# Hybrid state space and sparse attention block: the gated projection in another order, all state space products ahead of the attention products

## The chip, the cores and the metric

The kernel runs on one core of a Trainium2 chip. The metric is the device time of one execution in microseconds (us). A profile of one execution shows, for every engine, when its instructions ran and what they waited for: TensorE (PE), VectorE (DVE), ScalarE (ACT), GpSimd (POOL), and SyncE (SP), which here issues all DMA transfers in one queue.

## The reference

One decoder block over 2048 tokens of width 1024. A state space branch (S5) and a sparse attention branch (an indexer picks 256 keys per query) start from the same normalised input. Their outputs, 512 wide each, are projected to 1024, gated, added and projected again; a SwiGLU feed-forward part follows.

```python
y_ssm = _s5_branch(u, ...)                       # 2048 x 512
y_att = _dsa_branch(q, k, v, qi, ki, wi)         # 2048 x 512
g_ssm, g_att = jnp.split(gates, N_BRANCH, axis=-1)
merged = (jax.nn.sigmoid(g_ssm) * (y_ssm @ w_proj_ssm[l])
          + jax.nn.sigmoid(g_att) * (y_att @ w_proj_attn[l]))
x = x + merged @ w_out[l]
h2 = _rms(x, norm2_g[l])
x = x + (jax.nn.silu(h2 @ w_ffn_gate[l]) * (h2 @ w_ffn_up[l])) @ w_ffn_down[l]
```

## The kernel before

**Who sets the order.** Three Python generators write the program: `state` (the state space branch), `attention` (16 query tiles of 128, with the top-k search ahead of them) and `dense` (everything behind the branches). `Pace.run` asks whichever can go on first by its own model of the engines, so the three are woven into one order for each engine. That order is fixed when the program is built; at run time each engine takes its rows in that order and waits where a row needs another engine. All instructions are recorded by one helper, so the profile gives each of them line 206: they are told apart by the names of their tiles.

**Dense blocks.** `dense` handles four blocks (`tb` 0 to 3) of 512 tokens, each in `block`. Its stages are: the projection, 16 products of 12 matmuls (fp32 as a high and a low half, three matmuls for each of four depth slices), called P1 to P16 here; the output stage, `f<-ww,mg`, 192 matmuls; the normalisation and its turning (transposes `f<-ident,ha` and so on); then up, gate and down, `f<-h,ww` and `f<-wd,at`, 1664 matmuls. A product of the projection takes the ssm branch's tile `act0` or the attention branch's `act1` (four pieces of 512 KB each, stored to DRAM by the branches, loaded by `load_branch`) and a weight item `ww`. Before, a weight item holds the columns of one output tile for both branches. The products come in the order ssm, ssm, attention, attention for tiles 0 and 1, and then ssm and attention by turns.

**Merging.** For each product DVE multiplies the PSUM result with its gate (`scalar_tensor_tensor`, in the profile `g<-g,f`; called a scaling here). Gates `g0` and `g1` are loaded from DRAM (`g<-gate`, 256 KB), two buffers of each kind. Behind the second scaling of a tile, POOL or DVE adds the two (`g<-g,g`), ACT casts the high half (`mg<-g`) and DVE or POOL makes the low half (`mg<-g,mg`). The output stage reads `mg`: its k-th pair of tiles is first needed 12 k matmuls after its start.

**Weights.** Block 0 loads raw weights (`raw`, two buffers), ACT casts the high half, POOL or DVE makes the low half (`ww<-raw,ww`), and the pair is stored as `wc`. Blocks 1 to 3 load `wc` items (1 MB, `ww<-wc`) into four buffers; a load waits until TensorE has finished with the item that had the buffer.

**Attention and the blocks.** `self.attended` counts finished query tiles. Block `tb` waits, before it is written, until 4 (tb + 1) of them are finished. At the end of a block the next block's `act0` is loaded, and `act1` too if its attention is already finished; that is so for blocks 1 and 2, not for block 3.

**PSUM.** A block has a pool `psp` of 3 banks, and borrows 4 that attention leaves free at times (`spare_banks`, `bank`); the last block, when attention is over, has 8 of its own.

**DMA.** SP issues every transfer in program order and cycles through eight completion counters, so a transfer also waits for the one issued eight before it.

## Time and profile before

| | |
|---|---|
| median of three runs | 3360.59 us (3353.09 to 3363.12) |
| the profiled execution | 3357.88 us |
| its span, first to last instruction | 3355.8 us |
| TensorE busy in the span | 3171.5 us, 95% |
| DVE, ACT, POOL busy | 2106.4, 1275.1, 638.1 us (63%, 38%, 19%) |
| DMA, mean over the span | 180 GB/s |

The profiled execution is one run, so a sum of its parts is compared with its own 3357.88 us; the last 2 us are outside the span. A busy TensorE is not one at its peak: its instructions take longer when the clock granted to it is lower. In the rows below, a row of the timeline gives the start in us, the duration in us, the engine, the operation, the tiles written and read, how many such instructions stand together (xN), and in brackets how long the engine idled before it and on what it waited.

### The profile page before, as it was taken

The page shows a single profiled execution, that of the slowest core. Times are in us where ns is not written, and L with a number is a line of the kernel's source. Part 1 is how long each engine was busy: PE and PEld are TensorE (multiplying, and loading weights), DVE is VectorE, ACT ScalarE, POOL GpSimd, SP SyncE. Part 2 cuts the span into 40 slices and gives each one's busy share as a digit, 9 for nine tenths or more (in the row PEclk, how much of TensorE's full clock was granted, in tenths as well). Part 3 has the DMA queues.
Part 4 walks back from the last instruction along what each step waited for, and adds up shares of the span by engine and source line. Part 5 has one row for each costly group of instructions (what it writes and reads, how often), then busy time and mean ns, then how long its engine had stood idle before and what let it go on. Part 6 is the DMA issues. An engine that isn't in the chain of part 4 may idle for free. (4 is left out here: it accounts for less than half of the span.)

```text
span 3355.8 us, 42712 instructions
## 1 busy us (share of the span) xinstructions
PE 3171.5 (95%) x15528; PEld 2651.1 (79%) x15528; DVE 2106.4 (63%) x4532; ACT 1275.1 (38%) x2211; POOL 638.1 (19%) x628
## 2 busy tenths in 40 slices
PE   7999989899977999989999999999999999999999
PEld 6988767678755788877778888877888888788887
DVE  6555685555587766688687775876886666422223
ACT  3231544445552444346322443665314444210000
POOL 4323676522223311234100000001000000000000
PEclk9999999999988999999999999999999999999999
DMA  5743333534447775656847324366555332755543
GB/s 184 227 122 109 121 89 108 164 120 142 129 166 268 283 257 196 237 182 225 332 187 262 109 93 166 140 236 242 197 213 182 119 108 88 268 195 219 207 177 149
DMA packets 312961, 605.56 MB, mean 180 GB/s; under 512 B 46352, under 2 KB 194608, under 8 KB 282032
## 3 DMA queue, kind: packets, MB, share of 16 engines
q1 hardware_dynamic: 312752, 602.85, 51.7%
q8 instruction: 122, 2.00, 0.2%
q14 instruction: 87, 0.71, 0.1%
HBM read 434.70 MB, written 166.89 MB: 179 GB/s over the span
## 5 line engine op out<-in xcount | busy, mean ns | idle before, releaser
L206 PE MATMUL f<-h,ww 128*128 128x512 f32 (+1 forms) x4416 | 1013.1, 384 | 1.3 <-DVE h L206 0.8
L206 PEld LDWEIGHTS f<-h,ww 128*128 128x128 f32 x4416 | 803.4, 191 | 156.5 <-DVE h L206 1.8
L206 PE MATMUL f<-wd,at 128*128 128x512 f32 x2112 | 518.2, 397 | 28.7 <-DVE t L206 6.5
L206 PEld LDWEIGHTS f<-wd,at 128*128 128x128 f32 x2112 | 396.3, 191 | 116.5 <-DVE t L206 8.1
L206 PE MATMUL gps<-hT,gw 128*128 128x512 f32 x1536 | 387.5, 403 | 4.6 <-ACT gsg L206 3.2
L206 ACT ACTIVATE jka<-S,tr 128x1920 bf16<-128x1920 f32 (+6 forms) x217 | 305.6, 1408 | 180.5 <-DVE tr L206 128.7
L206 PEld LDWEIGHTS gps<-hT,gw 128*128 128x128 f32 x1536 | 288.3, 193 | 68.5 <-ACT gsg L206 5.2
L206 PE MATMUL mm<-w,hT 128*128 128x512 f32 (+1 forms) x1152 | 282.8, 403 | 10.3 <-DVE hT L206 7.2
L206 DVE TENSOR_TENSOR x<-f,x 128x512 f32<-128x512 f32 x352 | 235.1, 686 | 77.0 <-PE f L206 76.4
L206 PEld LDWEIGHTS mm<-w,hT 128*128 128x128 f32 x1152 | 241.5, 239 | 36.7 <-DVE hT L206 8.6
L206 DVE TENSOR_TENSOR tl<-pt,th 128x512 fp32r<-128x512 f32 (+1 forms) x288 | 183.8, 658 | 120.9 <-ACT th L206 119.8
L206 DVE SCALAR_TENSOR_TENSOR t<-t,f 128x512 f32<-128x512 f32 (+1 forms) x123 | 82.1, 668 | 271.8 <-PE f L206 223.6
L206 ACT CAST th<-pt 128x512 fp32r<-128x512 f32 (+1 forms) x288 | 155.5, 563 | 223.8 <-PE pt L206 220.2
L206 PE MATMUL f<-act,ww 128*128 128x512 f32 x768 | 191.8, 411 | 29.5 <-POOL ww L206 20.4
L206 PEld LDWEIGHTS f<-act,ww 128*128 128x128 f32 x768 | 151.2, 199 | 69.5 <-POOL ww L206 24.2
L206 POOL TENSOR_TENSOR g<-g,g 128x512 f32<-128x512 f32 x31 | 39.8, 1285 | 793.9 <-DVE g L206 793.9
L206 PE MATMUL f<-ww,mg 128*128 128x512 f32 x768 | 180.3, 397 | 10.6 <-ACT ww L206 7.0
L206 ACT ACTIVATE P<-P,m 128x1024 f32<-128x1024 f32 (+7 forms) x192 | 172.3, 900 | 46.9 <-DVE m L206 46.8
L206 PE MATMUL lg<-kk,q 128*128 128x512 f32 (+1 forms) x640 | 183.3, 388 | 3.5 <-DMA kk<-kk 3.5
L206 ACT ACTIVATE t<-f 128x512 f32<-128x512 f32 (+1 forms) x92 | 52.9, 575 | 343.8 <-PE f L206 343.7
L206 PEld LDWEIGHTS f<-ww,mg 128*128 128x128 f32 x768 | 147.2, 192 | 43.2 <-ACT ww L206 7.9
L206 ACT CAST at<-t 128x512 fp32r<-128x512 f32 (+1 forms) x92 | 55.2, 600 | 325.4 <-DVE t L206 325.3
(361 smaller groups left out, 4497.9 us busy)
## 6 DMA issues: line engine op xcount, KB each, us to landing
ww<-wc SPq DMA_DIRECT2D x180, 1024.0 KB, 4.9
wd<-wc SPq DMA_DIRECT2D x66, 1024.0 KB, 7.2
wc<-ww SPq DMA_DIRECT2D x60, 1024.0 KB, 7.5
raw<-in_w_in_dram SPq DMA_DIRECT2D x104, 256.0 KB, 3.4
wc<-wd SPq DMA_DIRECT2D x22, 1024.0 KB, 6.3
x<-in_x_dram SPq DMA_DIRECT2D x32, 512.0 KB, 5.3
gate<-gsg SPq DMA_DIRECT2D x64, 256.0 KB, 2.2
g<-gate SPq DMA_DIRECT2D x64, 256.0 KB, 5.7
```

Source lines behind the costliest of these rows:

```text
L206: return f(*args, **kw)
```

## The change

The weight items of the projection are regrouped: an item now holds two output tiles' columns of one branch, four items for the ssm branch and then four for the attention branch. The 16 products follow in that order: q = 0 to 7 are the ssm products, whose scalings write into `x1` (as `kept`), a tile that is free until the residual input is loaded into it; q = 8 to 15 are the attention products, each followed by its scaling, the addition of `kept`, and the split into `mg`. The wait for this block's attention moves from the block's start to q = 8; at its start a block only waits for the attention of the blocks before it. `act1`, where it has not been loaded before, is loaded at q = 6 if attention is finished when that place is written, else at q = 8. The loads of the residual `x1` move to q = 9, 11, 13 and 15. Every block has 3 own banks; once attention is over, the last block borrows 5 more, which `bank` gives out for short uses only. The depth of the ring of down weights, `nd`, is computed where the ring is made, with the same values.

```diff
--- before.py
+++ after.py
@@ -1663,11 +1663,12 @@
 
         a = self.a
         items = []
-        for ct in range(KD):
-            items.append(("w", lambda raw, ct=ct: [
-                (raw[:, i * 512:(i + 1) * 512].rearrange("p (k c) -> p k c", k=4),
-                 a[w][0, :, ct * 128:(ct + 1) * 128].rearrange("(k p) c -> p k c", p=128))
-                for i, w in enumerate(("w_proj_ssm", "w_proj_attn"))]))
+        for w in ("w_proj_ssm", "w_proj_attn"):
+            for c0 in range(0, KD, 2):
+                items.append(("w", lambda raw, w=w, c0=c0: [
+                    (raw[:, i * 512:(i + 1) * 512].rearrange("p (k c) -> p k c", k=4),
+                     a[w][0, :, (c0 + i) * 128:(c0 + i + 1) * 128].rearrange("(k p) c -> p k c", p=128))
+                    for i in range(2)]))
         for half in range(2):
             for q in range(4):
                 items.append(("w", lambda raw, half=half, q=q: [
@@ -1692,7 +1693,7 @@
             self.nc.sync.dma_start(z[:, :, k].bitcast(F32), (self.act_d, self.att_d)[br][tb][:, :, k])
         return z
 
-    def block(self, tb, bigp, ld, nps, nd):
+    def block(self, tb, bigp, ld):
 
         nc, a, at = self.nc, self.a, self.pace.at
         n = TB
@@ -1701,7 +1702,7 @@
         hf, h0 = t0 // HALF, t0 % HALF
         spare = self.pace.spare
         with ExitStack() as st:
-            psp = self.pool(st, "fps", nps, PSUM)
+            psp = self.pool(st, "fps", 3, PSUM)
             x1 = self.pool(st, "x1", 1).tile([128, nt, D], F32, name="x1")
 
             more, extra = ExitStack(), []
@@ -1744,34 +1745,49 @@
                     self.pace.tight = tb == 0
                     load_gate(0, 0)
                     act = self.act
-                    act += [self.load_branch(bigp, br, tb) for br in range(len(act), 2)]
+                    if not act:
+                        act.append(self.load_branch(bigp, 0, tb))
                     self.act = []
                     load_gate(1, 0)
-                    load_gate(0, 1)
-                    load_gate(1, 1)
-                    for q, (ct, br) in enumerate([(0, 0), (1, 0), (0, 1), (1, 1)] +
-                                                 [(ct, br) for ct in range(2, KD) for br in range(2)]):
-                        w = ld.get("w", 1 if q == 1 else 0)
-                        w = w.rearrange("p z a (b k c) -> p (z a) b k c", b=2, k=4)[:, :, br]
+
+                    kept = x1.rearrange("p t (a c) -> p (t a) c", a=2)
+                    for q in range(2 * KD):
+                        br, ct = q // KD, q % KD
+                        if q == KD:
+                            if self.attended < 4 * (tb + 1):
+                                yield lambda: at("PE") if self.attended >= 4 * (tb + 1) else ("PE", 1e9, None)
+                            if self.attended == NT:
+                                self.pace.BIAS = 0.0
+                                self.spare_banks = 5
+                        if q == KD - 2 or q == KD:
+
+                            if len(act) == 1 and self.attended >= 4 * (tb + 1):
+                                act.append(self.load_branch(bigp, 1, tb))
+                            if q < KD:
+                                load_gate(0, 1)
+                                load_gate(1, 1)
+                        w = ld.get("w")
+                        w = w.rearrange("p z a (b k c) -> p (z a) b k c", b=2, k=4)[:, :, ct % 2]
                         yield ready(w, act[br])
                         ps = bank()
                         for k in range(4):
                             self.mm3(ps, w[:, 0, k], w[:, 1, k], act[br][:, 0, k], act[br][:, 1, k], k == 0, k == 3)
                             ld.tick()
-                        x = gates[ct, br]
-                        nc.vector.scalar_tensor_tensor(x, x, 1.0, ps, op0=ALU.add, op1=ALU.mult)
-                        if br == 1:
+                        x = gates.pop((ct, br))
+                        if br == 0:
+                            nc.vector.scalar_tensor_tensor(kept[:, ct], x, 1.0, ps, op0=ALU.add, op1=ALU.mult)
+                        else:
+                            nc.vector.scalar_tensor_tensor(x, x, 1.0, ps, op0=ALU.add, op1=ALU.mult)
+                            spare(x).tensor_tensor(x, x, kept[:, ct], op=ALU.add)
+                            self.split(x, mg[:, 0, ct], mg[:, 1, ct], nc.scalar, spare(x))
+                        load_gate(ct + 2, br)
+                        if ct % 2 == 1:
                             ld.drop("w")
-                            x0, x = gates.pop((ct, 0)), gates.pop((ct, 1))
-                            spare(x0).tensor_tensor(x0, x0, x, op=ALU.add)
-                            self.split(x0, mg[:, 0, ct], mg[:, 1, ct], nc.scalar, spare(x0))
-                            load_gate(ct + 2, 0)
-                            load_gate(ct + 2, 1)
+                            if br == 1:
+                                t = ct // 2
+                                nc.sync.dma_start(x1[:, t], a["x"][0, t0 + t * 128:t0 + (t + 1) * 128])
                         if q == 3:
                             self.pace.tight = False
-                        if q in (4, 6, 8, 10):
-                            t = q // 2 - 2
-                            nc.sync.dma_start(x1[:, t], a["x"][0, t0 + t * 128:t0 + (t + 1) * 128])
                 fn = self.pool(sm, "fn", 1)
                 gB = fn.tile([128, D], F32, name="gB")
                 self.bcast_row(gB, a["norm2_g"], D)
@@ -1860,6 +1876,7 @@
                 self.pace.tight = False
             ap = self.pool(st, "fa", 5)
             tp = self.pool(st, "ft", 2)
+            nd = 2 if self.attended == NT else 1
             ld.ring("d", self.pool(st, "fd", nd), nd, 2)
 
             def gate(p):
@@ -1986,11 +2003,9 @@
                 for tb in range(NB):
                     if tb == 1:
                         first.close()
-                    yield lambda: self.pace.at("PE") if self.attended >= 4 * (tb + 1) else ("PE", 1e9, None)
-                    alone = self.attended == NT
-                    if alone:
-                        self.pace.BIAS = 0.0
-                    yield from self.block(tb, bigp, ld, *((8, 2) if alone else (3, 1)))
+                    if self.attended < 4 * tb:
+                        yield lambda: self.pace.at("PE") if self.attended >= 4 * tb else ("PE", 1e9, None)
+                    yield from self.block(tb, bigp, ld)
 
         st = ExitStack()
         pr = self.pool(st, "spr", 1)
```

TensorE has as many instructions as before; DVE has 9 more, ACT 4 more and POOL 13 fewer.

**Block 3 on SP.** Before, the last stores of attention (`att3`), a first gate, and the four loads of `act1` stand together, ahead of the block's fifth weight item `ww_25522<-wc4`:

```order
L206 DMA att3_189<-yh_25440 128x4x128 [waits DMAHW2_49,Activation_49]
L206 DMA att3_189<-ya_24339 128x4x128 [waits DMAHW3_49,DVE_49]
L206 DMA g0_25467<-gate0_1_135 128x512 [waits DMAHW4_49,PE_49]
L206 DMA act1_25469<-att3_189 128x2x512 [waits DMAHW5_49,DMAHW3_49,DMAHW2_49]
L206 DMA act1_25469<-att3_189 128x2x512 [waits DMAHW6_49]
L206 DMA act1_25469<-att3_189 128x2x512 [waits DMAHW7_49]
L206 DMA act1_25469<-att3_189 128x2x512 [waits DMAHW0_49]
L206 DMA g0_25474<-gate1_1_137 128x512 [waits DMAHW1_49]
L206 DMA g1_25476<-gate8_1_151 128x512
L206 DMA g1_25478<-gate9_1_153 128x512
L206 DMA ww_25522<-wc4_9257 128x2048 [waits DMAHW4_49,PE_49]
```

In the changed program the block has begun when attention ends. Around the same stores and loads SP's rows are these (gates of tiles 6 to 9, and the items `wc6` and `wc7`):

```order
L206 DMA g0_25540<-gate6_1_147 128x512 [waits DMAHW7_49,DVE_49]
L206 DMA g0_25559<-gate7_1_149 128x512 [waits DMAHW0_49,DVE_49]
L206 DMA ww_25561<-wc6_9259 128x2048 [waits PE_49]
L206 DMA g1_25563<-gate8_1_151 128x512
L206 DMA g1_25565<-gate9_1_153 128x512 [waits DMAHW6_49]
L206 DMA att3_189<-yh_25542 128x4x128 [waits Activation_49]
L206 DMA att3_189<-ya_24339 128x4x128
L206 DMA ww_25605<-wc7_9260 128x2048 [waits DMAHW1_49,PE_49]
L206 DMA act1_25607<-att3_189 128x2x512 [waits DMAHW7_49,DMAHW2_49,DMAHW0_49]
L206 DMA act1_25607<-att3_189 128x2x512 [waits DMAHW3_49]
L206 DMA act1_25607<-att3_189 128x2x512 [waits DMAHW4_49]
L206 DMA act1_25607<-att3_189 128x2x512 [waits DMAHW5_49]
```

The stores have moved behind the load of g0_25559, which waits for DVE (the scaling of P6 frees its buffer), and the `act1` loads behind ww_25605, which waits for TensorE to finish P8.

**Block 1 on DVE.** Before, two scalings stand ahead of each low half `mg`, here for two of the middle tiles of the block:

```order
L206 TENSOR_TENSOR mg_14512<-g0_14574,mg_14512 128x512
L206 SCALAR_TENSOR_TENSOR g0_14597<-g0_14597,f_14639 128x512
L206 SCALAR_TENSOR_TENSOR g1_14599<-g1_14599,f_14654 128x512
L206 TENSOR_TENSOR mg_14512<-g0_14597,mg_14512 128x512
L206 SCALAR_TENSOR_TENSOR g0_14635<-g0_14635,f_14677 128x512
L206 SCALAR_TENSOR_TENSOR g1_14637<-g1_14637,f_14692 128x512
```

In the changed program's second half, with attention products only, these are the first four tiles:

```order
L206 SCALAR_TENSOR_TENSOR g1_14619<-g1_14619,f_14659 128x512
L206 TENSOR_TENSOR mg_14506<-g1_14619,mg_14506 128x512
L206 SCALAR_TENSOR_TENSOR g1_14621<-g1_14621,f_14678 128x512
L206 TENSOR_TENSOR mg_14506<-g1_14621,mg_14506 128x512
L206 SCALAR_TENSOR_TENSOR g1_14676<-g1_14676,f_14700 128x512
L206 TENSOR_TENSOR mg_14506<-g1_14676,mg_14506 128x512
L206 SCALAR_TENSOR_TENSOR g1_14695<-g1_14695,f_14719 128x512
L206 TENSOR_TENSOR mg_14506<-g1_14695,mg_14506 128x512
```

Each low half has moved between two scalings: a scaling now stands behind the low half of the tile before it.

**Block 0 on DVE, the top-k search.** Rows on `jkd`, `uf` and `tf` are the search of later query tiles, six rows an iteration. Before, in the middle of the projection, they lie between the scalings singly and in part iterations:

```order
L206 SCALAR_TENSOR_TENSOR g0_9500<-g0_9500,f_9598 128x512
L206 TENSOR_SCALAR jkd_7800<-H4_8577,tf2_7816 128x320
L206 SCALAR_TENSOR_TENSOR jkd_7800,cnt2_7815<-H4_8577,tf2_7816,jkd_7800 128x320
L206 SCALAR_TENSOR_TENSOR g1_9502<-g1_9502,f_9615 128x512
L206 TENSOR_TENSOR mg_9369<-g0_9500,mg_9369 128x512
L206 SCALAR_TENSOR_TENSOR g0_9588<-g0_9588,f_9643 128x512
L206 TENSOR_SCALAR jkd_7800<-H5_8579,tf2_7816 128x384
L206 SCALAR_TENSOR_TENSOR jkd_7800,cnt2_7815<-H5_8579,tf2_7816,jkd_7800 128x384
L206 TENSOR_SCALAR uf2_7817<-cnt2_7815 128x2
L206 SCALAR_TENSOR_TENSOR tf2_7816<-uf2_7817,tf2_7816 128x2
L206 SCALAR_TENSOR_TENSOR g1_9590<-g1_9590,f_9662 128x512
L206 TENSOR_TENSOR g0_9588<-g0_9588,g1_9590 128x512
```

In the changed program five iterations stand together between the last ssm scaling (`x1_9352<-g0_9530,f_9564`, 31 rows above these) and the first attention scaling. This is the fifth, and what follows it:

```order
L206 TENSOR_SCALAR jkd_7800<-H4_8577,tf2_7816 128x320
L206 SCALAR_TENSOR_TENSOR jkd_7800,cnt2_7815<-H4_8577,tf2_7816,jkd_7800 128x320
L206 TENSOR_SCALAR jkd_7800<-H5_8579,tf2_7816 128x384
L206 SCALAR_TENSOR_TENSOR jkd_7800,cnt2_7815<-H5_8579,tf2_7816,jkd_7800 128x384
L206 TENSOR_SCALAR uf2_7817<-cnt2_7815 128x2
L206 SCALAR_TENSOR_TENSOR tf2_7816<-uf2_7817,tf2_7816 128x2
L206 SCALAR_TENSOR_TENSOR g1_9537<-g1_9537,f_9623 128x512
L206 TENSOR_TENSOR mg_9356<-g1_9537,mg_9356 128x512
L206 SCALAR_TENSOR_TENSOR g1_9539<-g1_9539,f_9648 128x512
L206 TENSOR_TENSOR g1_9539<-g1_9539,x1_9352 128x512
```

The search rows have moved out from between the scalings and stand in one stretch ahead of the attention half.

## Rows read from the trace of the kernel before

**Rows 1.** Waits of TensorE over the whole span by what it waited for: us in total, times, longest us.

```profile
PE f L206 <- POOL ww L206: 23.9, 11, 9.5
PE f L206 <- ACT ww L206: 11.8, 5, 4.6
PE f L206 <- DMA act<-att: 4.4, 4, 2.1
```

**Rows 2.** Busy time by stretch, for the projection of blocks 0, 1, 2 and 3. Columns: stretch, its length, busy us (and instructions) of PE, PEld, DVE, ACT and POOL, granted clock as a share of full speed, DMA share, GB/s.

```profile
980.80:1051.70 70.90, 55.35 (x192) 40.43 (x192) 51.46 (x111) 16.21 (x24) 29.23 (x16) 0.87 0.86 292
1621.90:1665.60 43.70, 43.70 (x194) 36.18 (x193) 15.94 (x25) 5.64 (x9) 9.02 (x7) 1.00 0.94 361
2247.30:2291.00 43.70, 43.70 (x194) 36.18 (x193) 15.68 (x23) 4.35 (x7) 9.01 (x7) 1.00 0.91 342
2884.90:2942.20 57.30, 51.08 (x203) 40.62 (x202) 18.14 (x28) 4.97 (x8) 8.98 (x7) 0.91 0.82 296
```

**Rows 3.** Timeline of PE from the end of block 2 to the output stage of block 3.

```profile
2879.31 5.62 PE L206 MATMUL f<-wd,at 128*128 128x512 f32 x24
...
2886.81 1.97 PE L206 MATMUL lg<-r,hsel 8*128 8x128 f32 x8 [1.78 <-DVE r L206]
2888.71 8.25 PE L206 MATMUL f<-act,ww 128*128 128x512 f32 x24
2898.07 0.96 PE L206 MATMUL f<-act,ww 128*128 128x512 f32 x3 [1.12 <-DMA act<-att]
...
2904.28 37.94 PE L206 MATMUL f<-act,ww 128*128 128x512 f32 x159 [0.36 <-DMA act<-att]
2942.06 3.11 PE L206 MATMUL f<-ww,mg 128*128 128x512 f32 x13
```

**Rows 4.** Timeline of SP, which issues the transfers, at the start of block 3.

```profile
2890.19 0.38 SPq L206 DMA_DIRECT2D att<-yh  x1
...
2893.90 2.50 SPq L206 DMA_DIRECT2D act<-att  x4
```

**Rows 5.** Timeline of PE in block 0's projection and output stage.

```profile
980.81 5.53 PE L206 MATMUL f<-act,ww 128*128 128x512 f32 x12 [9.54 <-POOL ww L206]
...
1020.57 5.30 PE L206 MATMUL f<-act,ww 128*128 128x512 f32 x22 [0.58 <-POOL ww L206]
...
1056.29 0.79 PE L206 MATMUL f<-ww,mg 128*128 128x512 f32 x1 [4.57 <-ACT ww L206]
...
1074.57 37.03 PE L206 MATMUL f<-ww,mg 128*128 128x512 f32 x155 [1.93 <-POOL ww L206]
```

**Rows 6.** Busy time of the first part of block 0's projection, columns as in rows 2.

```profile
980.80:1020.00 39.20, 31.23 (x98) 22.20 (x98) 26.81 (x60) 10.89 (x17) 16.17 (x9) 0.80 0.90 312
```

**Rows 7.** Timeline of DVE in block 3's projection: a scaling, the low half behind the second scaling of a tile, the next scaling.

```profile
2909.62 0.69 DVE L206 SCALAR_TENSOR_TENSOR g<-g,f 128x512 f32<-128x512 f32 x1 [0.19 <-PE f L206]
2912.42 0.69 DVE L206 TENSOR_TENSOR mg<-g,mg 128x512 fp32r<-128x512 f32 x1 [2.12 <-ACT mg L206]
2913.03 0.68 DVE L206 SCALAR_TENSOR_TENSOR g<-g,f 128x512 f32<-128x512 f32 x1
```

**Rows 8.** The gate tiles of block 1 (projection and output stage): time of their transfers from issue to landing.

```profile
DMA to landing us min/median/max: 2.8/6.2/7.5
```

**Rows 9.** Timeline of DVE in block 1's projection.

```profile
1659.89 1.31 DVE L206 SCALAR_TENSOR_TENSOR g<-g,f 128x512 f32<-128x512 f32 x2 [0.97 <-DMA g<-gate]
1663.32 0.69 DVE L206 TENSOR_TENSOR mg<-g,mg 128x512 fp32r<-128x512 f32 x1 [2.12 <-ACT mg L206]
1665.00 1.34 DVE L206 SCALAR_TENSOR_TENSOR g<-g,f 128x512 f32<-128x512 f32 x2 [0.99 <-DMA g<-gate]
```

**Rows 10.** Timeline of PE in the turning of the normalised rows and the first up product, of block 1 (the first two rows) and of block 3 (the last two): where the turning starts, and the first matmuls after it.

```profile
1709.88 1.09 PE L206 MATMUL f<-ident,ha 128*128 128x128 f32 x8 [0.75 <-DVE ss L206]
...
1723.12 12.21 PE L206 MATMUL f<-h,ww 128*128 128x256 f32 x80
...
2985.58 1.03 PE L206 MATMUL f<-ident,ha 128*128 128x128 f32 x8
...
2994.50 15.71 PE L206 MATMUL f<-h,ww 128*128 128x256 f32 x102
```

**Rows 11.** Timeline of SP at the start of block 0.

```profile
979.66 4.94 SPq L206 DMA_DIRECT2D act<-att  x4
984.83 2.06 SPq L206 DMA_DIRECT2D g<-gate  x3
987.29 0.38 SPq L206 DMA_DIRECT2D raw<-in_w_proj_ssm_dram  x1
```

**Rows 12.** Timeline of POOL in block 0's projection: a low half of weights and an addition of two scaled products.

```profile
1002.34 2.35 POOL L206 TENSOR_TENSOR ww<-raw,ww 128x1024 fp32r<-128x1024 f32 x1
1004.64 1.29 POOL L206 TENSOR_TENSOR g<-g,g 128x512 f32<-128x512 f32 x1
```

**Rows 13.** Timeline of DVE in the search: the same operation in two iterations that follow on each other, and in one beside POOL's row of 1002.34 us.

```profile
969.69 0.30 DVE L206 TENSOR_SCALAR jkd<-H,tf 128x320 bf16<-128x320 uint16 x1
...
972.17 0.30 DVE L206 TENSOR_SCALAR jkd<-H,tf 128x320 bf16<-128x320 uint16 x1
...
1002.33 2.47 DVE L206 TENSOR_SCALAR jkd<-H,tf 128x320 bf16<-128x320 uint16 x1
```

## The prediction, made before the changed kernel was timed

> **What bounds the kernel now.** I read four views, in this order. First the page: TensorE is busy 95% of the span, so only what makes TensorE wait can pay. Second, TensorE's waits by cause: of the waits that this change could touch, 23.9 us are for weights that POOL splits, 11.8 us for weights that ACT casts, and only 4.4 us for the attention branch's tiles [rows 1]. Third, the projection stage of each of the four blocks [rows 2]. Blocks 1 and 2 take 43.70 us with TensorE busy for 43.70 of them: nothing is waited for, and 43.70 / 192 = 0.2276 us is one matmul at full rate. Block 0 takes 70.9 us and block 3 57.3 us. Fourth, the timeline of those two.
>
> In block 3 attention ends just as block 2 does: its last rows stand at 2886.81 us, the first 24 matmuls of the projection take 8.25 us, the four pieces of the attention tile then let three matmuls through at a time, and from 2904.28 us all runs through [rows 3]. From 2884.9 us (2879.31 + 5.62) to 2942.06 us that is 57.2 us for 192 x 0.2276 = 43.7 us of products and some 1.5 us of attention: **about 12 us are lost there**, the largest loss that the change addresses. The tile's loads are issued at 2893.90 us, after attention's stores at 2890.19 us [rows 4], and the first products that need it start at 2898.07 us, the last piece is there at 2904.28 us [rows 3]: 4.2 us from first issue to first use, and 6.2 us from the first piece to the last.
>
> In block 0 the projection starts at 980.81 us, behind a wait of 9.54 us, is half done (98 matmuls) at 1020.0 us [rows 5, 6], and the stage that follows is free of weight waits from 1074.57 us on [rows 5].
>
> **Block 3: the wait moves.** The new order puts P1 to P8 (the ssm products) ahead of the attention tile. They start at 2884.9 us, take 96 x 0.2276 = 21.9 us and let attention's last eight matmuls in (1.97 us in [rows 3], about 1 us at full rate): P8 ends near 2907.9 us. What the order of SP shows decides the rest. Attention's stores now stand behind the gate load g0_25559, which waits for a result of P6, and the tile's loads behind ww_25605, which waits for P8 to release its weights. So they can't be issued before 2907.9 us, 14 us later than now. The first piece is usable 4.2 us later, or 2.9 us more when the 1 MB of ww_25605 goes ahead (1.05 MB at the 361 GB/s of [rows 2]): 2912.1 to 2915.0 us. The last piece comes 6.2 us behind, P9 ends 0.9 us after that, at 2919.2 to 2922.1 us, and seven products of 2.73 us end P16 at 2938.3 to 2941.2 us, against 2942.06 us [rows 3]: -0.9 to -3.8, and I take **-2**. The idle time ahead of P9 becomes one wait of 4 to 7 us in place of several short ones. The first 12 matmuls of block 0 took 5.53 us behind their 9.54 us wait [rows 5], 0.461 us each, the lower of the two clock levels (1.2 and 2.4 GHz); against 0.2276 that is 2.8 us more. P9 is paced by the pieces anyway, so I charge none of it; if P10 pays it, the term is +0.8.
>
> The Trainium skill speaks against the change here: "TensorE: Matmul & The Clock Gate", section "HAM oscillation — how this bites in real kernels", says that matmuls that come in bursts with a transfer waited for between them fall back to the slow clock and pay at each burst. By that rule block 3's term is the +0.8; the trace agrees in kind, by the 5.53 us of [rows 5].
>
> **Attention half, blocks 1 to 3: a chain in place of cover.** Now DVE scales two products per output tile, and POOL's addition, ACT's cast and DVE's low half follow once per 24 matmuls (5.46 us). In the new order that chain follows each of P9 to P16, every 2.73 us, and DVE's next scaling stands behind the low half of the one before. From one scaling to the next that order takes 3.41 us (2909.62 to 2913.03 us) [rows 7]. The gate tiles add to it: two buffers serve the attention half, and a tile is free only after the low half, so two products take max(6.82, 3.41 + L), where L is a gate load: 2.8, 6.2 and 7.5 us (least, median, most) in block 1 [rows 8], where scalings already wait for gates [rows 9]. The eighth merged tile is then ready 3 x max(6.82, 3.41 + L) + 6.9 us after P9. TensorE hides it until P16's end (7 x 2.73 = 19.1) and 39 matmuls of the output stage (8.9): 28.0 us. With L = 2.8 that is 27.4 us, no loss; with 6.2 it is 35.7 us, a loss of 7.7. L was measured while DMA moved 361 GB/s [rows 2]; the new chain spreads the same 2 MB over 7.9 us in place of 5.46, so I take L = 4.5: 30.6 us, a loss of 2.6, with a slower clock behind it **+3 in each of the three blocks**. Blocks 1 and 2 have no wait to set against it. The scalings of the ssm half write elsewhere and free their gate at once, so their two buffers take 0.7 + L per two products: with L = 6.2 that is 1.4 us behind per pair, 4.3 us by the last, less than the two products (5.46 us) by which three banks let TensorE run ahead.
>
> **Last block's banks.** Own banks go from 8 to 3, and the five borrowed ones serve neither the turning of the normalised rows nor the first up product. That passage takes 8.9 us in block 3 now (2985.58 to 2994.50) and 13.2 us in block 1 (1709.88 to 1723.12), which has 3 own banks and the search beside it [rows 10]. So 0 to +4.3; I take **+2**, as half of block 1's difference looks like the search.
>
> **Block 0.** The ssm half no longer stands behind the attention tile's loads, which now hold SP from 979.66 us for 4.94 us and put the next raw weights at 987.29 us [rows 11]. It is also rid of POOL's share in the merging, one addition of 1.29 us per output tile and at times a low half; the weights' own low halves, 2.35 us twice per item, fit into 5.46 us of products [rows 12]. P1 to P8 could then end at 980.81 + 5.53 + 84 x 0.2276 + some 6 us of remaining weight waits (an estimate) = 1011.5 us instead of 1020.0, and P9 starts at about 1016, when its tile has come behind the last ssm gates. But the order of DVE puts five iterations of the top-k search between the last ssm scaling and the first attention scaling: 2.48 us each when alone (969.69 to 972.17), 2.2 us more for each POOL split that meets one (2.47 against 0.30 us) [rows 13], so 12.4 to 16.8 us. The first attention scaling so falls at 1026 to 1030 us, and eight tiles of 3.4 us or more end at 1054 to 1058 us. The weights, all of which must still be split, hold the output stage as now. At best its last item starts at 1058, 16 us before 1074.57 us [rows 5], and the search that was left behind takes 2 back: -14. At worst the late merging costs more than the front gave, +3. I take **-5**, nearer to the worse end since [rows 1] names the weights.
>
> The added instructions themselves cost nothing on TensorE (as many as before); DVE has 9 more, ACT 4 more, POOL 13 fewer.
>
> **Sum.** -5 + 3 + 3 + (3 - 2 + 2) = +4 on the profiled 3357.9 us: 3361.9 us. That execution lies 2.7 us under the median of 3360.59 us, by less than the sum is good for; the forecast is **3362 us, no measurable change**. A measurement here tells 0.3% from nothing, 10 us to each side: 3350.5 to 3370.7.
>
> **Rivals.**
> 1. *Faster: block 0 keeps its front.* If the weight split follows the faster start, block 0 gives -14, and with L below 3.4 us the chain costs nothing: 3357.9 - 14 - 2 + 2 = 3344 us. For it: POOL was busy for only 29 of block 0's 71 us [rows 2]. Against it: the search on DVE. Chance 0.24, with block 3's tile coming early as a lesser way.
> 2. *Slower: the gate loads set the pace.* With L at 6.2 us or more the attention half loses 7.7 us in each of three blocks: 3357.9 - 5 + 3 x 7.7 - 2 + 2 = 3376 us. It decides from L = 5.5 us, where the three losses come to 17 us. For it: the median of [rows 8] lies above that. Against it: a stalled TensorE asks for less. Chance 0.28.
> 3. *Nothing but the place of the wait.* Block 3 loses before P9 what it lost before P1, blocks 0 to 2 break even: 3358 us. Within the forecast's bounds, 0.12 of its 0.46.
> 4. *The clock falls in block 3's long wait*: +2.8, 3365 us, 0.1 of the 0.46. With late banks as well it goes over 3371, 0.02, counted as slower.
>
> **How the numbers follow.** Forecast and its variants 0.46; faster 0.24; slower 0.28 + 0.02 = 0.30. The outermost tenth on each side is left out: 3344 to 3378 us, from the first rival to a little past the second. The forecast's own range is 3352 to 3370.
>
> **What would show it.** Block 3: loads of the attention tile issued after 2907 us and a wait of 4 to 7 us ahead of P9; wrong if they are issued before P8's end. Blocks 1 and 2: the output stage waits for the merged tiles on DVE or ACT, 1 to 5 us, and scalings 3.4 us or more apart; wrong if the output stage waits for nothing. Block 0: P8's end near 1012 and the last weight wait of the output stage near 1067 instead of 1074.57 us. The prediction fails if the search after block 0, once shifted, holds attention 4 to 7 back, or if waits appear in the feed-forward products, of which I assumed no change.

## The result, and the profile after

The changed kernel takes 3384.84 us (median of 4 runs, 3383.59 to 3389.05) beside 3357.55 us for the kernel before: ratio 1.0083, 95% interval 1.0063 to 1.0102. It is slower by 27 us; the forecast was 3362 us, 3344 to 3378, so the measured time lies above the whole range. The profiled execution took 3384.3 us, 26.4 us above that of before. TensorE's work is the same (15528 matmuls, 3171.0 us busy against 3171.5), so all of it is waiting.

Where it went, read from the starts of TensorE's rows in both timelines (a stage ends where the next one's first matmul starts):

| us, changed less before | forecast | measured |
|---|---|---|
| start of block 0 | 0 | +1.1 |
| block 0: projection | | -11.6 |
| its output stage | | +10.9 |
| its turning, up to the first uninterrupted up products | | +7.5 |
| the rest of block 0 | | +1.2 |
| block 0 in all | -5 | +7.9 |
| block 1 | +3 | +5.7 |
| block 2 | +3 | +5.3 |
| block 3: projection, from the end of block 2's down products | -2 | +0.6 |
| block 3: output stage | +3 | +4.2 |
| block 3: turning, with fewer own banks | +2 | +1.4 |
| sum | +4 | +26.3 |

The projection of the four blocks in the windows view (stretch, its length, busy us of PE, PEld, DVE, ACT and POOL, granted clock, DMA share, GB/s), to be set beside [rows 2]:

```profile
981.90:1042.80 60.90, 49.34 (x192) 37.70 (x192) 31.46 (x88) 12.98 (x19) 22.90 (x11) 0.87 0.89 306
1631.00:1674.70 43.70, 43.70 (x193) 36.20 (x194) 13.70 (x25) 7.28 (x11) 6.42 (x5) 1.00 0.74 270
2262.10:2305.80 43.70, 43.70 (x194) 36.19 (x193) 13.07 (x24) 7.19 (x9) 6.42 (x5) 1.00 0.75 268
2904.90:2962.90 58.00, 48.40 (x203) 38.16 (x202) 15.89 (x25) 3.73 (x6) 6.49 (x6) 0.91 0.71 247
```

In this stage blocks 1 and 2 are as before and block 0 is 10 us shorter: only in block 3 does the stage whose order was changed lose anything itself. TensorE's timeline in block 3 (start, duration, xN, and in brackets the wait ahead):

```profile
2904.86 8.45 PE L206 MATMUL f<-act,ww 128*128 128x512 f32 x36
2913.24 1.11 PE L206 MATMUL lg<-r,hsel 8*128 8x128 f32 x8
2914.27 13.87 PE L206 MATMUL f<-act,ww 128*128 128x512 f32 x60
2937.24 3.15 PE L206 MATMUL f<-act,ww 128*128 128x512 f32 x6 [9.10 <-issue]
2940.56 21.88 PE L206 MATMUL f<-act,ww 128*128 128x512 f32 x90 [0.17 <-DMA act<-att]
...
2970.99 39.71 PE L206 MATMUL f<-ww,mg 128*128 128x512 f32 x168 [2.53 <-DMA ww<-wc]
```

P1 to P8 now run with one row of attention among them, as forecast; then TensorE stands for 9.10 us, where 4 to 7 were forecast. SP at that place:

```profile
2925.25 0.55 SPq L206 DMA_DIRECT2D att<-yh  x1
2925.84 0.58 SPq L206 DMA_DIRECT2D att<-ya  x1
2928.17 0.33 SPq L206 DMA_DIRECT2D ww<-wc  x1
2932.80 2.49 SPq L206 DMA_DIRECT2D act<-att  x4
```

The loads (`act<-att`) are not issued when P8 releases its weights (`ww<-wc`, 2928.17 us) but 4.6 us later: they wait for attention's stores (`att<-yh`, `att<-ya`), issued at 2925.25 and 2925.84 us and landed at 2932.0 and 2932.8 us, 6.8 to 6.9 us after issue. TensorE's row names no releaser (`issue`); the first piece of the tile landed at 2937.16 us, and the matmuls start at 2937.24 us. Before, the same stores were issued at 2890.19 and the loads that wait for them at 2893.90 us [rows 4].

The clock falls behind the wait. Stretches ahead of it and behind it, columns as above:

```profile
2914.30:2928.10 13.80, 13.80 (x61) 11.15 (x60) 4.65 (x7) 0.62 (x1) 0.00 (x0) 1.00 0.83 298
2937.20:2940.50 3.30, 3.15 (x6) 1.67 (x6) 0.00 (x0) 0.00 (x0) 0.00 (x0) 0.50 0.99 342
2940.50:2946.00 5.50, 5.44 (x19) 4.28 (x20) 0.69 (x1) 0.42 (x1) 1.28 (x1) 0.76 0.07 25
2946.00:2962.50 16.50, 16.44 (x73) 13.29 (x71) 6.38 (x10) 2.69 (x5) 5.12 (x4) 1.00 0.65 234
```

From full clock ahead of the wait TensorE falls to 0.50 (1.2 GHz), and in the last stretch it is back at 1.00. P9 to P16 take 25.5 us in place of 21.85, but most of that is not the clock's price. P9's matmuls start in threes as the four pieces of the tile land, at 2937.16, 2938.70, 2940.52 and 2941.80 us (the row of 2940.56 us waits for the third). At full clock P10 could have started at 2941.80 + 3 x 0.2276 = 2942.5 us (an estimate from these rows); it started at 2943.24 us. So the slow clock cost about 0.7 us, and the pieces, against a tile that is there whole, about 2.5 us. The Trainium skill ("TensorE: Matmul & The Clock Gate", section "HAM oscillation — how this bites in real kernels") says that TensorE falls back to the slow clock behind such a wait for a transfer. The trace agrees with that.

Block 1. The projection waits for nothing; the wait comes later, in the output stage, and again at the turning (PE, then SP, then DVE from the first scaling of the attention half on):

```profile
1674.64 5.60 PE L206 MATMUL f<-ww,mg 128*128 128x512 f32 x24
1683.60 39.93 PE L206 MATMUL f<-ww,mg 128*128 128x512 f32 x168 [3.35 <-DMA ww<-wc]
1725.57 1.09 PE L206 MATMUL f<-ident,ha 128*128 128x128 f32 x8 [2.04 <-DVE ha L206]
```

```profile
1674.69 3.73 SPq L206 DMA_DIRECT2D g<-gate  x2
1678.51 0.38 SPq L206 DMA_DIRECT2D ww<-wc  x1
```

```profile
1656.91 0.69 DVE L206 SCALAR_TENSOR_TENSOR g<-g,f 128x512 f32<-128x512 f32 x1 [1.99 <-DMA g<-gate]
1659.71 0.69 DVE L206 TENSOR_TENSOR mg<-g,mg 128x512 fp32r<-128x512 f32 x1 [2.11 <-ACT mg L206]
1660.32 0.68 DVE L206 SCALAR_TENSOR_TENSOR g<-g,f 128x512 f32<-128x512 f32 x1
...
1684.28 0.69 DVE L206 TENSOR_TENSOR mg<-g,mg 128x512 fp32r<-128x512 f32 x1 [2.09 <-ACT mg L206]
```

In the attention half a scaling follows the one before after 3.41 us where no gate is late, as forecast from [rows 7]: DVE idles 2.1 us for ACT's cast in each. The last merged tile is there at 1685.0 us, 10.3 us behind the projection. But TensorE does not wait for it: it waits for a weight item whose load stands in SP's queue behind a gate load that itself waits for a merged tile.

Block 0, TensorE from P9 to the turning:

```profile
1018.00 4.11 PE L206 MATMUL f<-act,ww 128*128 128x512 f32 x9 [10.59 <-DMA act<-att]
...
1058.82 0.79 PE L206 MATMUL f<-ww,mg 128*128 128x512 f32 x1 [8.65 <-ACT ww L206]
...
1092.60 4.99 PE L206 MATMUL f<-ww,mg 128*128 128x512 f32 x12 [1.97 <-DVE ww L206]
1098.35 13.65 PE L206 MATMUL f<-ww,mg 128*128 128x512 f32 x59 [0.75 <-DVE ww L206]
1111.83 1.03 PE L206 MATMUL f<-ident,ha 128*128 128x128 f32 x8
1119.66 2.31 PE L206 MATMUL f<-ident,hb 128*128 128x128 f32 x8 [6.79 <-DVE x L206]
```

The front is 9 us ahead of before at the end of the projection (1042.84 against 1051.72 us) and level again at the turning (1111.83 against 1111.44 us): 2.93 us at 1045.77 us go to a PSUM bank that a scaling on DVE still holds, the rest to weights that are split too late, 8.65 us in one wait where [rows 5] had 4.57, and the last as late as 1098.35 us.

### The profile page after: what moved, and what is told of

Same layout as the page of the kernel before. It is cut to its first block, busy times and chain, and to the rows that moved or that the text cites. A ratio compares the mean times of both kernels' runs of the same rounds, so it can differ in the third digit from the quotient of the medians.

```text
span 3382.1 us, 42712 instructions
## 1 busy us (share of the span) xinstructions
PE 3171.0 (94%) x15528; PEld 2649.4 (78%) x15528; DVE 2105.8 (62%) x4541; ACT 1279.4 (38%) x2215; POOL 617.6 (18%) x615
## 5 line engine op out<-in xcount | busy, mean ns | idle before, releaser
L206 PE MATMUL f<-act,ww 128*128 128x512 f32 x768 | 184.2, 401 | 31.9 <-DMA act<-att 11.2
L206 PE MATMUL f<-ww,mg 128*128 128x512 f32 x768 | 188.1, 406 | 27.3 <-DMA ww<-wc 9.4
L206 POOL TENSOR_TENSOR g<-g,x 128x512 f32<-128x512 f32 x29 | 37.1, 1279 | 813.7 <-DVE g L206 813.7
```

Of the source, the lines that this page charges most:

```text
L206: return f(*args, **kw)
```

## The experiments

All runs, each with the kernel before on the same chip:

| run | median us | before there | ratio, interval |
|---|---|---|---|
| e1 pairs in block 0 | 3376.86 | 3358.06 | 1.0060, 1.0045 to 1.0075 |
| e2 four gates in blocks 1, 2 | 3382.07 | 3358.06 | 1.0078, 1.0061 to 1.0095 |
| e3 stores first | 3383.36 | 3358.06 | 1.0084, 1.0067 to 1.0101 |
| e4 pairs in all blocks | 3364.31 | 3358.06 | 1.0022, 1.0010 to 1.0033 |
| e5 low half later in 1, 2 | 3369.81 | 3357.39 | 1.0031, 1.0020 to 1.0043 |
| e6 low half later in all | 3360.23 | 3357.39 | 1.0007, 0.9998 to 1.0016 |
| e7 finish at once | 3379.92 | 3357.39 | 1.0067, 1.0053 to 1.0081 |
| e8 new order in block 3 alone, mended | 3346.46 | 3357.39 | 0.9974, 0.9964 to 0.9985 |
| e9 new order in all, mended | 3359.59 | 3358.79 | 1.0003, 0.9994 to 1.0011 |
| e10 the same, pairs in block 0 | 3350.54 | 3358.79 | 0.9973, 0.9962 to 0.9984 |
| e11 search between block 0's products | 3356.97 | 3355.76 | 1.0002, 0.9992 to 1.0012 |
| e12 more of it | 3360.24 | 3355.76 | 1.0012, 1.0001 to 1.0023 |
| e13 turning without search | 3348.20 | 3354.99 | 0.9977, 0.9968 to 0.9987 |
| e14 weights first in block 0 | 3351.47 | 3354.99 | 0.9988, 0.9977 to 1.0000 |

**The order itself.** Pairs put two ssm products and two attention products in turn, for two output tiles at a time; the weight items, the waits and the banks stay those of the changed kernel.

```diff
+turns = [0, 4, 1, 5, 2, 6, 3, 7] + list(range(8, len(items)))   # weights()
-br, ct = q // KD, q % KD
+br, ct = q // 2 % 2, q // 4 * 2 + q % 2                          # lead 2 for KD
```

e1, in block 0 alone:

> The changed kernel with block 0's products in pairs again (two ssm products, then two attention products of the same tiles); blocks 1 to 3 as changed. Theory A: the 8 to 9 us by which block 1 starts late come from the new order of block 0, because the search stands behind the late merging on DVE and takes the output stage and the turning with it. Then P16 ends near 1052 us again instead of 1042.8, the turning's 6.8 us wait on DVE goes, block 1 starts at 1622 to 1625 us, and the kernel takes 3375 to 3378 us. Rival B: the loss stems from how later attention falls into block 0's feed-forward part, which any change of order shifts: block 1 still starts at 1628 us or later, 3382 to 3386 us.

e4, in all four:

> The changed kernel with products in pairs in all four blocks: weight items by branch, ssm results kept in x1, 3 own banks in the last block and the late load of the attention tile remain, only the order of the products is near that of before. Theory A: the order alone made the kernel slower: 3355 to 3362 us, block 0 near before's times, output stages of blocks 1 and 2 at 43.6 us, block 3 about 1 to 2 us longer than before for its 3 banks. Rival B: what remains costs by itself (banks, items, merging into x1): 3366 us or more.

e1: block 0's output stage is 2.3 us longer than before in place of 10.9; the part behind it stays 9.9 us longer, and 8 us of the 27 come back. Block 0's projection keeps its gain with pairs: from P1 to the output stage it takes 64.7 to 67.0 us in e1, e4, e8 and e10, beside 63.8 in the changed kernel and 75.5 before, although in e1 the attention tile's loads are issued at the block's start again (from 977.40 us). So most of that gain is not the order's; another part of the change brings it (the weight items by branch are a candidate), and no run separates them.

e4: the output stages with the turning of blocks 1 and 2 are at +0.1 and +0.6 us, so their loss is the separation of the halves. Block 3's projection then costs 10.6 us more than before, counted from P1: with pairs TensorE stands for the attention tile early, 15.53 us. The median, 6 us above the kernel before, lies between the two theories, and these 10.6 us are more than the whole difference.

**Blocks 1 and 2: gates or merging?** e2 gives both branches four common gate buffers; e5 adds to e2 that a tile's low half follows the next scaling, with the addition always on POOL (the cast stays on ACT).

```diff
-gates[ct, br] = gp.tile([128, n], F32, name=f"g{br}")            # 2 of each
+gates[ct, br] = gp.tile([128, n], F32, name="g")                 # 4 in all
 scalar_tensor_tensor(x, x, 1.0, ps, ...)
+while late: late.pop()()                                         # e5: the tile before
-self.split(x, mg[:, 0, ct], mg[:, 1, ct], nc.scalar, spare(x))
+nc.scalar.copy(mg[:, 0, ct], x); late.append(low half on DVE)
```

> The changed kernel with the four gate buffers of blocks 1 and 2 shared by both branches (as much memory as two and two), so that a gate load of the attention half no longer waits for the low half of the tile before last. Theory A: in blocks 1 and 2 the output stage waits for a weight load that stands on SP behind such a gate load. Then the wait of 3.35 us after the output stage's first 24 matmuls goes, the stage takes 43.6 to 45 us in both blocks, and the kernel gains 8 to 11 us: 3374 to 3377 us. Rival B: the merging itself (scaling, addition, cast, low half, 3.4 us a tile in one line on DVE) is late: the wait turns into one for mg of 1.5 us or more per block, the gain is under 6 us: 3379 to 3385 us.

> The kernel with four shared gate buffers in blocks 1 and 2 (the run before this one of that name), and in the attention half of these two blocks DVE's low half of a tile is written into the program behind the next tile's scaling, with the addition always on POOL: DVE then need not wait for addition and cast between two scalings. Theory A: what blocks 1 and 2 lose is the late end of the merging on DVE (8.9 us behind P16 with four gate buffers, 3.5 in the kernel before) and the search that stands behind it; the loss only shows up at the turning. Then the merging ends 3 to 4.5 us behind P16, output stage and turning of blocks 1 and 2 come back to before's times within 1 us each, and the kernel takes 3371 to 3376 us. Rival B: the turning waits for something else (residual loads that came late, 3 own banks that were always there): the merging ends early and the turning still waits 5 us or more, 3380 to 3385 us.

TensorE in block 1, of e2 and then of e5:

```profile
1675.42 43.68 PE L207 MATMUL f<-ww,mg 128*128 128x512 f32 x192
1725.06 1.97 PE L207 MATMUL f<-ident,ha 128*128 128x128 f32 x8 [5.95 <-DVE ss L207]
```

```profile
1672.90 43.68 PE L208 MATMUL f<-ww,mg 128*128 128x512 f32 x192
1716.91 1.09 PE L208 MATMUL f<-ident,ha 128*128 128x128 f32 x8 [0.34 <-DVE ss L208]
```

e2 took away every wait of the output stage (192 matmuls in 43.68 us) and gained little, 1.3 and 2.5 us of the 6.5 and 6.9 us that output stage and turning had lost in the two blocks: 5.95 us appear at the turning, where DVE's normalisation stands behind the search, and the search behind the late merging. e5 removed DVE's idle time in the merging, and both waits are gone (output stage with the turning 0.4 us shorter than before in both blocks). The wait for weights was the sign, DVE's serial merging the cause. The late low half was run only together with the four gates and the addition on POOL, so the share of each is not shown.

**Block 3: stores or attention's end?** The generator of attention pauses ahead of its last steps until the model that writes the order has their tiles ready. e3 drops the pause ahead of the last query tile's stores; e7 drops all three pauses of that tile, and lets `act1` be loaded from P3 on.

```diff
-yield at("SP", yh, ya)
+if i < NT - 1: yield at("SP", yh, ya)      # e3; e7 also for the waits on PE and ACT ahead of it
+if q == 2 and tb == NB - 1 and len(act) == 1 and self.attended == NT: act.append(load)   # e7
```

> The changed kernel with the last stores of attention issued as soon as they are written into the program, so that on SP they stand ahead of the last ssm gate and the seventh weight item, and the loads of the attention tile ahead of the eighth. Theory A: the 9.1 us wait ahead of P9 in block 3 is SP's order: stores ready near 2921 us are issued at 2925 and land at 2932.8, and the loads wait for that. Then the loads start near 2924.5 us, P9 near 2929 to 2931 us instead of 2937.2, and the kernel gains 6 to 8 us: 3377 to 3379 us. Rival B: the transfers are bound by DMA bandwidth, shared with weights and gates: the pieces land at 2938 us or later all the same, gain under 3 us: 3382 to 3385 us.

> The changed kernel in which the last steps of attention's last query tile are written into the program at one place, ahead of block 3's first product (as they stood before), and the attention tile's loads are issued at P3, when its stores have landed. Theory A: block 3 loses because products P1 to P3 stand ahead of attention's last matmuls on TensorE and its stores stand behind gates and weights on SP. Then TensorE waits about 2 us at the start, no wait stands ahead of P9, P16 ends 46 to 48 us after block 2's end instead of 57.9, and the kernel gains 8 to 11 us against the changed one: 3373 to 3377 us. Rival B: the tile's transfers or the gates are late anyway because DMA is shared: gain under 4 us, 3381 to 3385 us.

e3: the stores go out at 2923.33 us, land after 4.5 us, the loads follow at 2928.35 us, and the first matmul of P9 starts 27.4 us behind the first of P1, against 32.4 us: 5.0 us come back in the first half, and the second half, from P9 to the output stage, takes 1.5 us longer (27.0 against 25.5), so block 3's projection gains 3.5 us. The kernel's time shows nothing of it (ratio 1.0084 beside 1.0083), so by the time alone rival B would have been right; by the trace it is theory A, with less than its full gain and 4.10 us of the wait left. e7: attention's matmuls stand ahead of P1 again (a wait of 1.78 us), the loads are issued at 2920.1 us, nothing waits ahead of P9 any more, and the one wait of the stage is 1.15 us ahead of P8, for a bank. The kernel gains some 5 us by the medians, between the two theories, and the intervals of its ratio and the changed kernel's overlap. So the wait of 9.10 us is the path stores, landing, loads: shortened in e3, gone in e7.

**All mends.** e6 is e5 in all four blocks. e8 has pairs in blocks 0 to 2 and the new order in block 3 alone, with the edits of e5 and e7. e9 has the new order in all blocks with these edits, e10 the same with pairs in block 0.

> As the run above, in all four blocks. Theory A: in block 0 too, DVE's waits inside the merging (about 2.1 us a tile) hold back the search behind it; without them the search of block 0 ends 8 to 14 us earlier than in the changed kernel, block 1 starts 6 to 12 us earlier, block 3 loses 3 to 5 us less behind P16, and the kernel takes 3358 to 3368 us. Rival B: block 0 is held by the splitting of weights and by the search's own length, so block 1 starts within 3 us of the changed kernel: 3368 to 3375 us.

> Pairs of products in blocks 0 to 2, the new order in block 3 alone, with all that the other runs point to: attention's last steps at one place, its tile loaded at P3, four shared gate buffers, the low half behind the next scaling. Theory A (each block's loss has the causes named so far): block 3 starts about where it did in the kernel before or up to 3 us earlier, its projection takes 46 to 48 us in place of 57.3, its output stage 43.6 to 44.5, the rest 1.3 us longer for its banks: 3345 to 3352 us, 6 to 13 us faster than the kernel before. Rival B: gains ahead of the feed-forward part are taken back by what runs beside it, or blocks 0 to 2 lose again: 3355 us or more.

> The changed kernel's order in all four blocks, with the mends of the runs before: four shared gate buffers, the low half behind the next scaling with its addition on GpSimd, attention's last tile finished and stored at once, and the attention tile of block 3 loaded from P3 on. Against the run with pairs in blocks 0 to 2 it differs in the order of those three blocks alone. Theory A (block 0's new order itself costs, since the search that it leaves behind the merging delays attention 4 to 7 and with it the feed-forward part): block 1 starts 7 to 10 us later than in the run with pairs, blocks 1 and 2 take about 1 us less each, and the median is 3351 to 3357 us. Theory B (with the merging out of DVE's way block 0's order costs nothing, and what was seen there is scatter between programs): block 1 starts within 3 us of the run with pairs, and the median is 3343 to 3349 us.

> The run e9, with pairs in block 0 alone; blocks 1 to 3 keep the changed kernel's order with all mends. Theory A (block 0's new order is what is left of the loss): 7 to 10 us under e9, block 1 starts where it did in the run with pairs in blocks 0 to 2, and the median is 3344 to 3348 us, under the kernel before. Theory B (nothing hangs on block 0's order): within 3 us of e9.

Block 3 of e8:

```profile
2882.32 1.31 PE L209 MATMUL lg<-r,hsel 8*128 8x128 f32 x8 [1.77 <-DVE r L209]
2883.56 45.57 PE L209 MATMUL f<-act,ww 128*128 128x512 f32 x192
2928.96 43.69 PE L209 MATMUL f<-ww,mg 128*128 128x512 f32 x192
```

The 192 matmuls of the projection take 45.57 us with no wait among them. From P1 to the output stage block 3 is 7.9 us shorter than before: the waits for the attention tile [rows 3] are gone. e8 beats both kernels, by 11 us and, by the ratios, 37 us. No run has these mends with pairs in block 3, so how much of the 11 us the mends alone would give is not shown.

e6 came out in theory A's range of 3358 to 3368 us, but not by its cause: block 1 starts 649.6 us behind block 0's first matmul, 649.1 in the changed kernel, as rival B had it; of what e6 gains over e5, 4.3 us are block 3's output stage (43.5 us in place of 47.8). e9 is level with before and e10 is as far below it as e8: what the new order still costs, some 10 us, hangs on block 0, the only place in which e9 and e10 differ. The theory that this was mere scatter has fallen. Both medians lie above the ranges of theory A. In the two profiles block 1 starts 4.9 us earlier in e10, seen from block 0's first matmul; the rest of the 10 us is not located.

**Block 0: the search left behind?** The search's last result came at 161.5 us after block 0's first matmul in e9 and at 152.6 us before. e11 delays each product by 2 us in the model that writes the order (e12 by 5), so that search rows stand between them.

```diff
+need = ready(w, act[br])
+yield (lambda: (need()[0], max(need()[1], self.pace.free["PE"]) + 2.0, None)) if tb == 0 else need
-yield ready(w, act[br])
```

> The run e9 (the changed kernel's order in all blocks, with all mends), and in block 0 each product of the projection stands 2 us later in the model that writes the order. So the search stands between block 0's products again: 10 of its row pairs more in the ssm half, and 6 pairs fewer behind the projection; the products themselves keep the changed kernel's order. Measured from block 0's first matmul, the search's last result stood at 152.6 us in the kernel before, 152.1 with pairs, 161.5 in e9; block 1's first matmul at 641.1, 639.0 and 648.1. Theory A (block 0's loss is the search that the new order leaves behind): the search ends at 150 to 157 us, block 1 starts at 640 to 645 us, median 3351 to 3356 us. Theory B (the late search is a mere companion; the order of weights and tiles costs): block 1 starts at 647 us or later, median 3358 to 3364 us.

> The run e11 with 5 us in place of 2: still more of the search stands in the ssm half. Theory A: the search's last result at 148 to 156 us behind block 0's first matmul, block 1 within 3 us of e11, the front slower by what the search takes from the scalings; median 3350 to 3357 us. Theory B: block 1 starts at 647 us or later, 3358 to 3366 us.

My theory fell. The search's last result came at 144.6 us in e11 (1124.0 - 979.4) and 123.8 us in e12, earlier than I had expected and than before; block 1 started at 646.9 and 652.9 us, where e9 had 648.2. In the runs up to then an early end of the search and an early start of block 1 had gone together; e11 shows that the first does not bring the second. Its edit moves more than the search: from the first up product to the first down product block 0 takes 88.4 us in e11 and 75.1 in e9. What sets the start of block 1 is not shown. e12's median lies in theory B's range, e11's between the two.

**Block 0: the weights behind the merging?** In the changed kernel ACT and SP, ahead of the 8.65 us wait, have these rows:

```profile
1047.07 0.62 ACT L206 CAST mg<-g 128x512 fp32r<-128x512 f32 x1 [3.47 <-POOL g L206]
1053.82 0.62 ACT L206 CAST mg<-g 128x512 fp32r<-128x512 f32 x1 [6.14 <-POOL g L206]
1057.20 0.62 ACT L206 CAST mg<-g 128x512 fp32r<-128x512 f32 x1 [2.76 <-POOL g L206]
1057.72 1.04 ACT L206 CAST ww<-raw 128x1024 fp32r<-128x1024 f32 x1
```

```profile
1041.56 0.47 SPq L206 DMA_DIRECT2D raw<-in_w_out_dram  x1
...
1044.35 4.41 SPq L206 DMA_DIRECT2D g<-gate  x2
...
1055.19 3.70 SPq L206 DMA_DIRECT2D g<-gate  x2
...
1061.22 0.38 SPq L206 DMA_DIRECT2D raw<-in_w_out_dram  x1
```

ACT's cast of a weight item (1057.72 us), whose raw tile landed at 1041.76 us, stands behind merging casts; each of these waits for an addition behind a scaling on DVE, and some scalings wait for a gate (3.29 us at 1051.70). Until the weight's low half is made no raw buffer is free, and for 19.7 us no raw weights are loaded. e14 is e9 with the split of an item, where one is at hand, written ahead of each merging in block 0.

```diff
+if tb == 0 and q >= KD and ld.here and ld.room(): ld.split()
 x = gates.pop((ct, br))
```

> The run e9 (the changed kernel's order in all blocks, with all mends), and in block 0 a weight item's split is written ahead of each merging of an attention product, where one is at hand, so that ACT's casts of two items no longer stand behind all eight merging casts. Theory A (block 0's output stage loses its 10 to 12 us because the weight splits stand behind the merging in the same queues, and the loads of raw weights behind the splits): the output stage takes 3 us or more less than e9's 66.1 us, and block 1 starts earlier by as much. Theory B (the weights are late for another reason, such as the buffers they are written to): the output stage within 2 us of 66.1, median 3357 to 3362 us.

```profile
1061.55 20.94 PE L208 MATMUL f<-ww,mg 128*128 128x512 f32 x84 [2.28 <-POOL ww L208]
...
1101.01 1.03 PE L208 MATMUL f<-ident,ha 128*128 128x128 f32 x8
1108.63 2.31 PE L208 MATMUL f<-ident,hb 128*128 128x128 f32 x8 [6.58 <-DVE x L208]
```

From 1038.99 to 1061.53 us raw loads now follow every 6.7 to 8.2 us, the output stage takes 60.8 us in place of e9's 66.1, block 1 starts 6.0 us earlier, seen from block 0's first matmul, and the kernel is 0.15% faster than e9 by the ratios, whose intervals just overlap. So the weights behind the merging hold the output stage: shown for half of its 11 us.

**Block 0: the turning.** In the rows of the changed kernel, and of e14 above, TensorE waits 6.6 to 6.8 us for the last residual additions on DVE (0.56 before); ahead of them on DVE stands a piece of the search of 7.4 us (1111.56 to 1118.92). e13 is e8 without the yields among the last products of the output stage, so that no search row stands there.

```diff
-yield ready(w, mg) if q == 0 else at("PE", w)
+if not (tb == 0 and half == 1 and t == nt - 2): yield ready(w, mg) if q == 0 else at("PE", w)
```

> The run with pairs in blocks 0 to 2 and the mended new order in block 3, and one edit more in block 0: behind the second group of normalised rows no row of the search may stand ahead of the last residual additions and the turning. The feed-forward part of block 0 was 8.7 to 12.3 us longer than before in every run so far but one, whatever order its projection had; in the profiles TensorE waits 5.8 to 6.8 us there for the last residual additions on DVE, which stand behind a piece of the search of 7.3 us. Theory A (that position is the loss): the wait falls under 1.5 us, the part behind the output stage takes 5 to 8 us less than in the run it is built on, median 3339 to 3343 us. Theory B (the search's piece, moved behind, holds attention 4 to 7 back by as much): the wait is gone but block 1 starts within 2 us of where it did, median 3345 to 3349 us.

```profile
1098.38 0.60 PE L209 MATMUL f<-ident,hb 128*128 128x128 f32 x4
1102.87 1.01 PE L209 MATMUL f<-ident,hb 128*128 128x128 f32 x4 [3.89 <-DVE h L209]
...
1115.63 1.97 PE L209 MATMUL f<-ident,hh 128*128 128x128 f32 x8 [6.31 <-DVE h L209]
```

That wait (6.51 us in e8) is gone, one of 3.89 us has come, and the one ahead of the last transposes has grown from 5.07 to 6.31 us; the turning is 2.2 us shorter than in e8 and block 1 starts 5.6 us later, seen from block 0's first matmul (644.7 and 639.0 us), so neither theory holds. The median is level with e8's. Why the part behind the output stage takes 7.2 to 12.3 us longer than before in every run, with pairs too, stays open; what is shown is that neither the place of that piece nor the end of the search decides it alone.

## Why the prediction was wrong

**Block 0 (-5 forecast, +7.9).** The front came near the forecast in its times: P8's end at 1007.4 us (near 1012), P9 at 1018 us (1016), P16's end 9 us ahead of before, the first attention scaling at 1031.37 us (1026 to 1030). That was in part luck, since e1 has the same gain without the reason given for it. The output stage did not: its last weight wait was forecast near 1067 us in place of 1074.57, and came at 1098.35 us. The step that failed is "the weights, all of which must still be split, hold the output stage as now", with its worst case of +3. The splits share ACT, DVE and SP's queue with the merging, and I had moved the merging onto them in one stretch: +10.9 us where I had the output stage end earlier. Of these 10.9 us, 5.3 come back with the splits ahead of the merging [e14]; the rest is open. I also assumed no change in the feed-forward part, which gave its turning no term: it is 7.5 us longer, behind a piece of the search, and why that time does not come back when the piece is moved [e13] stays open. The other search sign that I named, a late end that holds attention 4 to 7 back, is not the cause as far as e11 tells: an early end did not bring block 1 forward.

**Blocks 1 and 2 (+3 each, +5.7 and +5.3).** The chain itself came as forecast, 3.41 us a tile: in block 1 the eighth merged tile was ready 29.2 us after P9's end, 30.6 forecast, and the gate loads issued within the attention half landed in 2.5 to 3.9 us where I took 4.5. The step that failed is the price, "TensorE hides it until P16's end (7 x 2.73 = 19.1) and 39 matmuls of the output stage (8.9): 28.0 us". By that rule 29.2 us cost 1.2 us; output stage and turning lost 6.5 and 6.9 us, of which the rest of the two blocks gave back 0.8 and 1.7. I counted only what stood over the last use of the merged tiles; but other work waits behind it in order, the weight load on SP and the search and normalisation on DVE, so the slip of DVE shows later and whole. The forecast that the output stage waits for merged tiles was wrong: it waits for weights. Rival 2, the gate loads, names a cause that e2 excludes as the main one, and its 3376 us is too short as well.

**Block 3's projection (-2, +0.6).** The failing step is that the loads stand "behind ww_25605, which waits for P8 to release its weights", as the last thing that holds them. The stores are on the path, and their landing had no term: the last landed 6.9 us after its issue, 4.6 us after the release. Rival 4, the slower clock behind the wait, came true in kind, at about 0.7 us for the 2.8 that it was given: P9 was paced by the pieces, as the forecast had said, so the clock is not the miss. (The "over 3371" of rival 4 does not follow from its terms: 3361.9 + 2.8 and 2.3 more for late banks are 3367 us.) Without that path the same stage gains 8.6 us, counted from block 2's end as in the table [e8].

**Output stage and banks of block 3 (+3 and +2, +4.2 and +1.4).** As forecast in kind and nearly in size.

The sum missed by 22 us: 13 in block 0, 5 in blocks 1 and 2, 3 in block 3, 1 at the start. The misses whose cause is shown have one shape: I moved work on a queue and priced it against its own reader, and not against what stands behind it or, in block 3, ahead of it. What stays open is the other 5.6 us of block 0's output stage, and why the 7.5 us of its turning do not come back.

## What to carry to other kernels

Where work is gathered into one stretch, price it by everything queued behind it on each in-order engine and on the DMA queue, not by its own consumer: the loss surfaces at an unrelated wait, and taking that wait away moves it on (3.35 us for weights became 5.95 us for a row sum). Where a transfer is moved back in its queue, follow its chain to the first store, landing times included. Two times that move together over many runs do not show a cause: move one of them alone, and read what else the edit has moved.

## What the runs showed that I had not expected

A store of 256 KB landed 6.8 us after its issue when a 1 MB weight load and two gate loads had been issued in the 1.4 us ahead of it, 4.5 us after it in e3, with one gate load in that stretch, and 2.4 to 2.9 us after it in the kernel before. One wait of 9.1 us took the granted clock from 1.00 to 0.50 for 3.3 us and to 0.76 for the next 5.5, and yet cost only about 0.7 us, since the first matmuls behind it were paced by their transfers anyway. The same order up to block 0 starts it at 975 to 982 us in different runs, so a difference of a few us in one profile is not read alone.
